# Background modulation steps of a hybrid encoder layer: from the gated recurrence's stage and the attention's projections to the first part of the output projection

## The chip, the core and the metric

The kernel runs on one core of a Trainium2 chip. A core has a matrix engine (TensorE, PE in the profile, with its weight loads listed apart as PEld), a vector engine (VectorE, DVE), an activation engine (ScalarE, ACT), a general engine (GpSimd, POOL) and a sync engine (SyncE, SP) that here only issues DMAs. The engines run side by side, each through its own instructions in order, and wait for each other by semaphores. The metric is the device time of one execution in microseconds; lower is better. A profile of one execution gives the start, length and waits of every instruction.

## The reference, cut to what matters

One encoder layer on 512 tokens of width 2048, in fp32. The input is modulated by a vector that is computed from a condition `c`, projected, mixed by four mixers of 512 channels each, projected back, and followed by a gated feed-forward network.

```
c_act = silu(c)
mod = c_act @ ada_w[l] + ada_b[l]                       # 2048 x 12288 weights, one row
shift1, scale1, gate1, shift2, scale2, gate2 = split(mod, 6)
h = x * (1 + scale1) + shift1
proj = h @ w_in[l]
o_a = _hgrn2(...)            # gated recurrence, 4 heads of 128
o_b = _s5(...)               # diagonal state space
o_c = _stick_breaking(...)   # attention, 4 heads of 128
o_d = _rwkv7(...)            # delta-rule recurrence, 8 heads of 64
mix = concatenate([o_a, o_b, o_c, o_d]) @ w_out[l]
x = layer_norm(ALPHA * x + gate1 * mix)
h = x * (1 + scale2) + shift2
ffn = (silu(h @ ffn_w1[l]) * (h @ ffn_w3[l])) @ ffn_w2[l]
x = layer_norm(ALPHA * x + gate2 * ffn)
```

The change concerns the part of `mod` that is needed late: `shift2` and `scale2`, which are used only when the feed-forward network begins.

## The kernel before, in words

**Matrix products.** Every fp32 product is done as three products of fp32r numbers: each operand is split into a high part (a cast on ACT, L102) and a low part (a subtraction on DVE, L105), and `mm3` (L592) adds high·high, low·high and high·low into one PSUM tile. A weight chunk is loaded by SP (`wr`), split into `wh` and `wl` by `wload` (L580), and used at once. A chunk of the projections is 128 rows by 512 columns; in the output projection it meets four token tiles, thus 12 matmuls of 128x512 for a chunk.

**Order.** The mixers' work and the projections are strung together by the string `ORDER` (L40). Each token names a piece of work. `K0` to `K3` are the attention's query and key projections of a head, `H0` to `H3` the heads of the gated recurrence, `L0` and `L1` the logarithms ahead of them, `VS` the attention's values, `A0` and `A1` its scores (tiles `sz`, `sl`, for two heads each), `TAIL` the end of the gated recurrence, `B0` and `B1` the attention's products with the values, `W1` and `W2` the first two parts of the output projection (`w_out`, L1420). A Tile scheduler places the instructions from this order, from priorities (`high_priority`, with 1500 ahead for the heads by `BEFORE`, L43, and 500 for the weight chunks, L582) and from its own estimate of when things are ready; so an instruction can stand well ahead of or behind its token.

**Background steps.** The product of `c_act` with three of the six parts of `ada_w` (in the order `gate1`, `scale2`, `shift2`, that is parts 2, 4, 3) is not a stage of its own. `ada_queue` (L1141) makes 12 items of it, a part's column block of 512 each. An item has 16 steps. A step loads a 128x512 tile `aw` of 256 KB (L1112, on SP's queue; the pool `ap` has three such tiles) and multiplies and adds it into `acc` on DVE (L123, or L118 for the first of an item). An item ends with `end` (L1123): it takes a PSUM tile `pd` from the four that the projections use too, does four matmuls of `acc` with a column of ones (128x1 each), and DVE writes the four columns into `mod`. This end is queued between later steps, at the tenth step of the item after the next, or behind ten empty entries for the last two. With them the queue has 224 entries.

**Rate.** The number behind the colon of a token is `E.rate`: so many entries of the queue are taken (`pump`, L1154) behind each weight chunk of that token (4 chunks for a feature tile, so 8 for `K0`; 16 for `VS`; 32 for `W1`, eight rows of `w_out` for each of four column blocks n). A load is issued up to three entries ahead. `PUMP` takes all that are left.

```
    while n and E.bg:
        for j in range(min(3, len(E.bg))):
            ld, do = E.bg[j]
            if ld:
                ld()
                E.bg[j] = (None, do)
        E.bg.pop(0)[1]()
        n -= 1
```

**The output projection.** `w_out` takes four PSUM tiles `pd` for a column block n, runs through the eight chunks, and then, for each token tile, DVE multiplies the PSUM tile by the gate (`go<-pd,g`) and adds it to the residual (`acc<-acc,go`). Since the pool has four `pd`, the next column block's matmuls wait for these `go`. Behind `W2` comes the last part, whose weights `wr` are loaded early, multiplied by the gate `g1` (L1468; `g1` lies in the pool `ap`, as `aw` does) and split (L1469).

Of the kernel before, what the change touches and what calls it, by code (L numbers as in the profile page):

```python
# [37 lines left out]
START = "M0 E0 G0 C0 g2 M1 S0 g6 F0 M2 S1 g1 E1"  # L38

ORDER = ("k3 xg:3 r1:1 v1 k2:1 v3 r3:3 v0:2 S5 r2 r0:1 KEYS SUB INV v2:3 V:1 R12:3 R4:3 CHAIN F2:1 F1:2 F3:1 "  # L40
         "R0:2 F0 K1:2 L0 H0 H1 K0:2 L1 H2 H3 VS:2 A0 K3:2 K2:2 PUMP TAIL B0 A1 W1:2 B1 W2")

BEFORE = {"S5": 600, "KEYS": 600, "SUB": 300, "INV": 1000, "CHAIN": 1500, "H": 1500}  # L43

# [1811 lines left out]
```

## Time and profile before

| | |
|---|---|
| three executions | 2540.97, 2546.42, 2553.87 us |
| median | 2546.42 us |
| the profiled execution, its own time | 2543.48 us |
| its span in the trace | 2541.5 us |
| granted TensorE clock, mean | 0.98 |
| instructions in the profile | 33306 |
| HBM read, written | 445.51 MB, 34.10 MB |

The profile's page gives busy time by engine, the span in 40 slices, and groups of instructions. Finer views of the same execution list single instructions in order of start (start and length in us, engine, line, operation, output<-inputs, and in square brackets the idle time just before and what ended it), or the busy time of each engine in chosen stretches. Matmuls are pipelined: a row of a matmul is listed with a length that overlaps the next one's start, so distances between starts tell its rate. The stretches that matter here are 712 to 834 us (the heads of the gated recurrence), 834 to 922 us (attention scores, the end of the recurrence, and the output projection's first column block) and 922 to 935 us (the step from its first to its second column block).

### The profile page before, as it was taken

The numbers are of one execution on the slowest core, as the hardware profiler recorded it, in microseconds if no ns is written. First come the engines' busy times: TensorE is split into PE (matmuls) and PEld (weight loads), VectorE is DVE, ScalarE is ACT, GpSimd is POOL, SyncE is SP. The second block draws the span as 40 slices with busy tenths as digits, with TensorE's granted clock in tenths as the row PEclk, the third lists the DMA queues.
The fourth block names the chain that finished last, engine by engine and source line by source line (L and its number), as shares of the span: only waits on it lengthen the run. The fifth ranks groups of instructions, "written<-read, shape, count | busy, mean of one in ns | idle before, by whom it ended". The sixth has DMA issues, their size and how long they took to land. (4 is left out here: it accounts for less than half of the span.)

```text
span 2541.5 us, 33306 instructions
## 1 busy us (share of the span) xinstructions
PE 2437.8 (96%) x11890; PEld 1897.7 (75%) x11890; DVE 1730.7 (68%) x2673; ACT 955.5 (38%) x1406; POOL 131.4 (5%) x293
## 2 busy tenths in 40 slices
PE   8999999999999999989999999999999999999996
PEld 3557767776788778867777877787778788788885
DVE  3755987357689975788787778777877744536227
ACT  2435242322454654164444444434443421121122
POOL 3300000010000000000000000000000000000000
PEclk9999999899999999999999999999999999999998
DMA  9876324334744554336666566655665788869632
GB/s 294 258 245 199 92 75 126 103 116 145 227 130 137 167 173 133 125 100 208 219 208 206 180 203 214 201 182 197 208 204 192 258 321 294 300 206 315 225 117 82
DMA packets 328877, 481.83 MB, mean 190 GB/s; under 512 B 44962, under 2 KB 151676, under 8 KB 328712
## 3 DMA queue, kind: packets, MB, share of 16 engines
q1 hardware_dynamic: 317976, 452.78, 55.3%
q0 software_dynamic: 8480, 26.27, 2.7%
q8 instruction: 93, 1.52, 0.3%
q10 hardware_dynamic: 2256, 0.67, 0.1%
q14 instruction: 72, 0.59, 0.1%
HBM read 445.51 MB, written 34.10 MB: 189 GB/s over the span
## 5 line engine op out<-in xcount | busy, mean ns | idle before, releaser
L102 ACT CAST wh<-wx 128x1024 fp32r<-128x1024 f32 (+1 forms) x416 | 401.2, 970 | 735.9 <-PE p L93 348.7
L105 DVE TENSOR_TENSOR wl<-wx,wh 128x1024 fp32r<-128x1024 f32 (+1 forms) x416 | 457.5, 1119 | 264.4 <-ACT wh L102 262.1
L102 ACT CAST wh<-wr 128x512 fp32r<-128x512 f32 x236 | 145.5, 618 | 329.2 <-PE pd L93 224.7
L123 DVE SCALAR_TENSOR_TENSOR acc<-aw,cact,acc 128x512 f32<-128x512 f32 x240 | 179.8, 749 | 123.6 <-DMA aw<-in_ada_w_dram 120.3
L93 PE MATMUL pt<-wl,gh 128*128 128x512 f32 x640 | 249.3, 390 | 2.1 <-DVE wl L105 1.8
L93 PE MATMUL pt<-wh,gh 128*128 128x512 f32 x640 | 249.1, 389 | 0.0
L93 PE MATMUL pt<-wh,gl 128*128 128x512 f32 x640 | 249.0, 389 | 0.0
L105 DVE TENSOR_TENSOR wx<-wx 128x512 f32<-128x512 f32 (+1 forms) x264 | 225.1, 866 | 28.6 <-DMA wx<-in_ffn_w_dram 26.9
L105 DVE TENSOR_TENSOR wl<-wr,wh 128x512 fp32r<-128x512 f32 x236 | 162.0, 689 | 113.3 <-ACT wh L102 96.2
L93 PE MATMUL pd<-hh,wl 128*128 128x512 f32 x512 | 205.6, 402 | 5.6 <-DVE wl L105 5.5
L93 PE MATMUL pd<-hh,wh 128*128 128x512 f32 x512 | 207.6, 407 | 2.4 <-ACT hh L102 2.4
L93 PE MATMUL pd<-hl,wh 128*128 128x512 f32 x512 | 204.0, 399 | 0.0
L93 PE MATMUL p<-wl,hdh 128*128 128x512 f32 x352 | 140.6, 404 | 20.0 <-DVE wl L105 20.0
L93 PE MATMUL p<-wh,hch 128*128 128x512 f32 x336 | 137.1, 408 | 16.4 <-DVE g L105 12.3
L93 PE MATMUL p<-wh,hdh 128*128 128x512 f32 x352 | 141.8, 403 | 1.1 <-ACT u L102 1.1
L93 PEld LDWEIGHTS pt<-wl,gh 128*128 128x128 f32 x640 | 120.1, 188 | 28.6 <-DVE wl L105 4.0
L93 PE MATMUL p<-wh,hdl 128*128 128x512 f32 x352 | 141.3, 402 | 0.0
L93 PEld LDWEIGHTS pt<-wh,gh 128*128 128x128 f32 x640 | 120.2, 188 | 25.6 <-ACT wh L102 0.8
L93 PEld LDWEIGHTS pt<-wh,gl 128*128 128x128 f32 x640 | 120.2, 188 | 25.1
L93 PE MATMUL p<-wl,hch 128*128 128x512 f32 x336 | 135.7, 404 | 0.3 <-DVE wl L105 0.3
L93 PE MATMUL p<-wh,hcl 128*128 128x512 f32 x336 | 135.0, 402 | 0.0
L93 PE MATMUL p<-wl,hbh 128*128 128x512 f32 x336 | 132.2, 393 | 0.8 <-DVE wl L105 0.8
(530 smaller groups left out, 4535.3 us busy)
## 6 DMA issues: line engine op xcount, KB each, us to landing
wx<-in_ffn_w_dram SPq DMA_DIRECT2D x592, 256.0 KB, 3.4
aw<-in_ada_w_dram SPq DMA_DIRECT2D x384, 256.0 KB, 4.6
wr<-in_w_in_dram SPq DMA_DIRECT2D x184, 256.0 KB, 3.3
wx<-in_ffn_w_dram SPq DMA_DIRECT2D x44, 1024.0 KB, 6.1
gh<-gd SPq DMA_DIRECT2D x88, 256.0 KB, 5.3
gl<-gd SPq DMA_DIRECT2D x88, 256.0 KB, 6.2
wr<-in_w_out_dram SPq DMA_DIRECT2D x64, 256.0 KB, 3.0
gd<-gh POOLq DMA_DIRECT2D x44, 256.0 KB, 4.1
```

What stands on the lines that cost most here:

```text
L93: return self.nc.tensor.matmul(out=out, lhsT=lhsT, rhs=rhs, start=start, stop=stop, **kw)
L102: self.nc.scalar.copy(out=out, in_=in_)
L105: self.nc.vector.tensor_tensor(out=out, in0=a, in1=b, op=op)
L123: self.nc.vector.scalar_tensor_tensor(out=out, in0=a, scalar=s, in1=b, op0=op0, op1=op1)
```

## The change

Only the string `ORDER` changes.

```diff
 ORDER = ("k3 xg:3 ... CHAIN F2:1 F1:2 F3:1 "
-         "R0:2 F0 K1:2 L0 H0 H1 K0:2 L1 H2 H3 VS:2 A0 K3:2 K2:2 PUMP TAIL B0 A1 W1:2 B1 W2")
+         "R0:2 F0 K1 L0 H0 H1 K0 L1 H2 H3 VS:1 A0 K3:1 K2:1 TAIL B0 A1 W1:4 PUMP B1 W2")
```

Up to `R0` both take 136 of the 224 entries. Before, `K1` and `K0` take 16 each, `VS` 32, `K3` 16, `K2` the last 8 (of 16 possible), so that `PUMP` and `W1` find the queue empty. After, `K1` and `K0` take none, `VS` 16, `K3` and `K2` 8 each, and the last 56 are taken by `W1`, four behind each of its first 14 chunks. These 56 are 32 steps with a load and a multiplication (the last two items, of `shift2`), the ends of four items, and 20 empty entries. `PUMP` finds nothing in either.

How the scheduler places it shows in the order of the instructions on each engine. The first place is DVE between the end of head 0 and the start of head 1 of the gated recurrence (`hS` and `ho` are head 0's last tiles, `hk`, `he`, `hlb` head 1's first, `acc<-aw` a background step, `wl` a weight chunk's low part). Before:

```order
L123 SCALAR_TENSOR_TENSOR acc_6611<-aw_6936,cact,acc_6611 128x512
L123 SCALAR_TENSOR_TENSOR hS_6753<-hS_6747,heb_6731,pm_6751 128x128
L123 SCALAR_TENSOR_TENSOR acc_6611<-aw_6939,cact,acc_6611 128x512
L123 SCALAR_TENSOR_TENSOR hS_6759<-hS_6753,heb_6731,pm_6757 128x128
L123 SCALAR_TENSOR_TENSOR acc_6611<-aw_6960,cact,acc_6611 128x512
L123 SCALAR_TENSOR_TENSOR ho_6763<-ho_6763,half_hg_norm_g,hgg_6402 128x512
L123 SCALAR_TENSOR_TENSOR acc_6611<-aw_6963,cact,acc_6611 128x512
L105 TENSOR_TENSOR wl_7045<-wr_7042,wh_7044 128x512
L123 SCALAR_TENSOR_TENSOR hk_6770<-hf_6016,he_6017 128x512
L123 SCALAR_TENSOR_TENSOR acc_6611<-aw_6984,cact,acc_6611 128x512
L123 SCALAR_TENSOR_TENSOR he_6017<-hf_6016,he_6017 128x512
L123 SCALAR_TENSOR_TENSOR acc_6611<-aw_6987,cact,acc_6611 128x512
```

The same place after:

```order
L105 TENSOR_TENSOR wl_6887<-wr_6884,wh_6886 128x512
L123 SCALAR_TENSOR_TENSOR hS_6701<-hS_6695,heb_6679,pm_6699 128x128
L123 SCALAR_TENSOR_TENSOR hS_6707<-hS_6701,heb_6679,pm_6705 128x128
L123 SCALAR_TENSOR_TENSOR ho_6711<-ho_6711,half_hg_norm_g,hgg_6402 128x512
L105 TENSOR_TENSOR wl_6905<-wr_6902,wh_6904 128x512
L123 SCALAR_TENSOR_TENSOR hk_6718<-hf_6016,he_6017 128x512
L123 SCALAR_TENSOR_TENSOR he_6017<-hf_6016,he_6017 128x512
L105 TENSOR_TENSOR hlb_6018<-hlb_6018,he_6017 128x512
L126 SCALAR_TENSOR_TENSOR hb_6724<-m_217,hlb_6018 128x512
```

The background steps between the head's instructions are gone, and the weight chunks' `wl` stand closer. Counted over the whole order on DVE, 28 background multiplications stand ahead of the first `hk` in the projections of `K1` and its neighbours before and 29 after, since the scheduler draws `VS`'s steps forward; about 32 stand among the four heads before and 3 after; about 17 stand from there to the second scores' `sz` before and 32 after; and from there none before and 16 after.

The second place is PE where `W1` goes from its first to its second column block (`pd` with `cath`, `catl` are the block's matmuls, each pair of `wh` and `wl` a weight chunk). Before:

```order
L93 MATMUL pd_8432<-wh_8561,cath_8411 128x512
L93 MATMUL pd_8432<-wh_8561,catl_8412 128x512
L93 MATMUL pd_8432<-wl_8562,cath_8411 128x512
L93 MATMUL pd_8603<-wh_8609,cath_8383 128x512
L93 MATMUL pd_8603<-wh_8609,catl_8384 128x512
L93 MATMUL pd_8603<-wl_8610,cath_8383 128x512
L93 MATMUL pd_8604<-wh_8609,cath_8383 128x512
```

And after, with the ends of two items and transposes of the scores (`pm<-ident,sz`) between:

```order
L93 MATMUL pd_8314<-wh_8535,cath_8293 128x512
L93 MATMUL pd_8314<-wh_8535,catl_8294 128x512
L93 MATMUL pd_8314<-wl_8536,cath_8293 128x512
L93 MATMUL pd_8400<-ones,acc_6395 128x1 x4
L96 MATMUL pm_9111<-ident,sz_8188 128x128 x4
L96 MATMUL pm_9118<-ident,sz_8189 128x128
L93 MATMUL pd_8527<-ones,acc_7657 128x1 x4
L93 MATMUL pd_8589<-wh_8595,cath_8265 128x512
L93 MATMUL pd_8589<-wh_8595,catl_8266 128x512
L93 MATMUL pd_8589<-wl_8596,cath_8265 128x512
L93 MATMUL pd_8589<-wh_8615,cath_8269 128x512
```

The two ends take the first two PSUM tiles that come free; the second block's first tile `pd_8589` now is the third to come free, where before its `pd_8603` was the first.

The third place is DVE at the same step, where the tiles come free. Before:

```order
L105 TENSOR_TENSOR go_8577<-pd_8429,g_1813_8427 128x512
L105 TENSOR_TENSOR go_8580<-pd_8430,g_1813_8427 128x512
L105 TENSOR_TENSOR acc_8415<-acc_8415,go_8577 128x512
L105 TENSOR_TENSOR wl_8646<-wr_8643,wh_8645 128x512
L105 TENSOR_TENSOR acc_8418<-acc_8418,go_8580 128x512
L105 TENSOR_TENSOR go_8583<-pd_8431,g_1813_8427 128x512
L105 TENSOR_TENSOR go_8586<-pd_8432,g_1813_8427 128x512
```

After, with the first two `go`, the end's `mod<-pd_8400` and a `wl` just ahead of these rows:

```order
L118 TENSOR_SCALAR acc_8462<-aw_8436,cact 128x512
L123 SCALAR_TENSOR_TENSOR mod<-pd_8527,c_148 128x4
L123 SCALAR_TENSOR_TENSOR acc_8462<-aw_8457,cact,acc_8462 128x512
L105 TENSOR_TENSOR acc_8297<-acc_8297,go_8563 128x512
L123 SCALAR_TENSOR_TENSOR acc_8462<-aw_8460,cact,acc_8462 128x512
L105 TENSOR_TENSOR acc_8300<-acc_8300,go_8566 128x512
L105 TENSOR_TENSOR go_8569<-pd_8313,g_1777_8309 128x512
L123 SCALAR_TENSOR_TENSOR acc_8462<-aw_8464,cact,acc_8462 128x512
L105 TENSOR_TENSOR acc_8303<-acc_8303,go_8569 128x512
L123 SCALAR_TENSOR_TENSOR acc_8462<-aw_8467,cact,acc_8462 128x512
L105 TENSOR_TENSOR go_8572<-pd_8314,g_1777_8309 128x512
```

The third and the fourth `go`, which free the second block's first two tiles, now stand behind two writes of `mod`, five background multiplications and three additions.

## The prediction

> **What bounds the kernel now.** I read the busy times of the engines first, then the busy time by stretch where the change works, then single instructions at the one place where PE stops.
>
> ```profile
> span 2541.5 us, 33306 instructions
> PE 2437.8 (96%) x11890; PEld 1897.7 (75%) x11890; DVE 1730.7 (68%) x2673; ACT 955.5 (38%) x1406; POOL 131.4 (5%) x293
> ```
>
> PE is busy for 96% of the span; a microsecond can be won only where PE idles or runs slowly, and is lost where the change makes PE wait. The sum is made against this execution's own time, 2543.48 us, of which 2541.5 are the span; the median of the three is 2.9 higher. The stretches (for each engine busy us and instructions, then granted clock, DMA share, GB/s):
>
> ```profile
> core 0: us, PE busy (x) PEld busy (x) DVE busy (x) ACT busy (x) POOL busy (x), PEclk, DMA share, GB/s
> 656.00:672.00 16.00, 13.52 (x57) 10.47 (x58) 10.70 (x18) 7.30 (x11) 0.00 (x0) 1.00 0.78 233
> 712.00:834.00 122.00, 119.94 (x697) 101.47 (x696) 109.02 (x214) 55.73 (x122) 1.58 (x3) 1.00 0.42 122
> 834.00:900.00 66.00, 63.69 (x309) 49.40 (x308) 58.91 (x107) 43.90 (x77) 0.00 (x0) 1.00 0.60 184
> 900.00:922.00 22.00, 21.90 (x97) 17.64 (x96) 19.95 (x37) 17.76 (x29) 0.00 (x0) 1.00 0.65 213
> 922.00:935.00 13.00, 7.86 (x25) 6.02 (x24) 10.18 (x20) 4.97 (x9) 0.00 (x0) 0.74 0.43 142
> 935.00:1040.00 105.00, 105.00 (x492) 86.96 (x491) 61.28 (x97) 39.64 (x68) 0.00 (x0) 1.00 0.38 123
> ```
>
> While the heads run (712 to 834), DVE is busy for 109 of 122 us, yet PE idles only 2.06. From 834 to 900 PE idles 2.31. From 935 on it does not idle at all. The loss is in 922 to 935, between `W1`'s first and second column block; PE there:
>
> ```profile
> 921.98 0.39 PE L93 MATMUL pd<-wl,cath 128*128 128x512 f32 x1
> 927.51 0.76 PE L93 MATMUL pd<-wh,cath 128*128 128x512 f32 x1 [5.14 <-ACT sz L99]
> 928.08 0.63 PE L93 MATMUL pd<-wh,catl 128*128 128x512 f32 x1
> ...
> 931.92 0.50 PE L93 MATMUL pd<-wh,catl 128*128 128x512 f32 x1
> 932.26 0.39 PE L93 MATMUL pd<-wl,cath 128*128 128x512 f32 x1
> 932.48 0.39 PE L93 MATMUL pd<-wh,cath 128*128 128x512 f32 x1
> ```
>
> PE waits 5.14 us and then runs at half rate: eleven starts, 927.51 to 932.26, take 4.75 us where at 0.227 each (932.26 to 932.48, like the rows before the pause) they would take 2.50, so 2.25 more are lost. The releaser is given as ACT's `sz`, but the rows of DVE show what came last:
>
> ```profile
> 920.15 2.36 DVE L126 TENSOR_TENSOR_SCAN sl<-ones,sl 128x512 f32<-128x512 f32 x3
> 922.47 0.69 DVE L105 TENSOR_TENSOR sz<-sz,sl 128x512 f32<-128x512 f32 x1
> 923.07 0.69 DVE L105 TENSOR_TENSOR wl<-wr,wh 128x512 fp32r<-128x512 f32 x1
> 923.67 2.50 DVE L105 TENSOR_TENSOR sz<-sz,sl 128x512 f32<-128x512 f32 x4
> 926.08 0.69 DVE L105 TENSOR_TENSOR wl<-wr,wh 128x512 fp32r<-128x512 f32 x1
> 926.68 1.29 DVE L105 TENSOR_TENSOR go<-pd,g 128x512 f32<-128x512 f32 x2
> ```
>
> The `go` that frees the first PSUM tile stands behind the scores' `sl` and `sz`, and 0.83 us after its start (926.68 to 927.51) the second block starts. DVE operations of 0.69 start 0.60 apart (922.47, 923.07, 923.67).
>
> **The change part by part.** No multiplication, load or end is removed; 192 stay 192 over the kernel. So only places count.
>
> *1. The serial chain between the column blocks.* After, the second block's first two tiles are the third and fourth to come free, because two ends take the first two. The prices:
>
> ```profile
> 708.79 0.95 PE L93 MATMUL pd<-ones,acc 128*128 128x1 f32 x8
> L96 PE MATMUL pm<-ident,sz 128*128 128x128 f32 x20 | 2.5, 272 | 0.0
> L123 DVE SCALAR_TENSOR_TENSOR mod<-pd,c 128x4 f32<-128x4 f32 x8 | 1.3, 158 | 2.2 <-PE pd L93 2.2
> L123 DVE SCALAR_TENSOR_TENSOR acc<-aw,cact,acc 128x512 f32<-128x512 f32 x28 | 20.9, 747 | 0.0
> L118 DVE TENSOR_SCALAR acc<-aw,cact 128x512 f32<-128x512 f32 x2 | 1.0, 482 | 0.0
> ```
>
> An end is 0.95 on PE (its four matmuls leave eight records) and 0.16 on DVE; five transposes are 2.5/20 x 5 = 0.6; a multiplication is 0.75, started 0.66 apart by the overlap above. A hand-over between the engines is 0.83 - 0.69 = 0.14. Counted from the start of the first `go`: the first end runs on PE 0.83 to 1.78; its `mod` on DVE 1.92 to 2.08; `wl` to 2.68; the first multiplication to 3.16. On PE the transposes run to 2.38, the second end to 3.33, so its `mod` to 3.63. Then two multiplications (1.32), two `acc` (1.20), the third `go` (0.69) and the hand-over (0.14): the second block starts at 7.0 instead of 0.83, 6.2 later. The two ends and the transposes (2.5) are work that PE had to do elsewhere before, where it is saturated, so **+3.7** net. Its second tile needs the fourth `go`, which ends two multiplications, one `acc` and itself behind the third: 1.32 + 0.60 + 0.60 = 2.5 later, while PE has five matmuls for the first tile (1.1): **+1.4**. The multiplications wait for loads as well, in order on DVE:
>
> ```profile
> DMA to landing us min/median/max: 2.6/3.5/4.6
> 668.40 0.75 DVE L123 SCALAR_TENSOR_TENSOR acc<-aw,cact,acc 128x512 f32<-128x512 f32 x1 [2.06 <-DMA aw<-in_ada_w_dram]
> ```
>
> With three tiles in the pool, the tile of the fourth multiplication is loaded once the first is done (3.16) and read at 7.0 - 0.14 = 6.9, 3.7 later: a load of 2.6 or 3.5 is in time, one of 4.6 adds 0.9. I leave it at 0, bounds 0 and +1.
>
> *2. The clock behind this pause.* Half rate behind the pause cost 2.25. A longer pause may cost the same again (0), or the ends and transposes are also at half rate and the ten matmuls behind the second wait too (2.5 + 2.25 = 4.7). What shows that a short pause does not count:
>
> ```profile
> 714.14 1.10 PE L93 MATMUL pm<-hx 128*128 128x64 f32 x8 [1.98 <-DVE hx L105]
> ```
>
> This pause of 1.98 lies in a stretch with a granted clock of 1.00. The second wait is 1.4, so it should be free by itself; I take **+1.5**, nearer to nothing, bounds 0 and +4.7. The Trainium skill, page "TensorE: Matmul & The Clock Gate", section "Part 1: The HAM clock gate (the "warmup" mystery)", has an activity window of about 3.4 us that runs free, at whose end an idle array falls to half rate and a busy one returns to full; the rows agree (5.14 us slowed it, 1.98 did not, and it came back after 4.75). By that rule the sum would lie between nothing and one further window.
>
> *3. The step from the second to the third block.* There the last two ends take the first two tiles. By the same prices: first `mod` to 2.08, `acc` to 2.68, second end on PE to 2.73, its `mod` to 3.03, `acc` to 3.63, third `go` to 4.32, hand-over 4.46, against 0.83; less 1.9 of ends: **+1.7**, bounds 0 (PE finds other matmuls) and +1.7. In the trace of before PE does not idle here (the row from 935).
>
> *4. The scores' stage, 834 to 922.* Some 32 multiplications instead of 17 stand there.
>
> ```profile
> L123 DVE SCALAR_TENSOR_TENSOR acc<-aw,cact,acc 128x512 f32<-128x512 f32 x17 | 12.7, 749 | 2.2 <-DMA aw<-in_ada_w_dram 2.2
> L123 DVE SCALAR_TENSOR_TENSOR acc<-aw,cact,acc 128x512 f32<-128x512 f32 x11 | 8.2, 750 | 5.3 <-DMA aw<-in_ada_w_dram 5.0
> L105 DVE TENSOR_TENSOR wr<-wr,g 128x512 f32<-128x512 f32 x9 | 6.1, 689 | 1.9 <-DMA wr<-in_w_out_dram 1.9
> ```
>
> These rows are the multiplications of 834 to 900, those of 656 to 672, and the gated weights of the last part in 900 to 922. Where 17 multiplications waited 2.2 us for loads, PE idled 2.31, or 0.136 each; where 11 waited 5.0, it idled 2.48, or 0.225 each. Behind a waiting multiplication stand the `wl` that PE needs. Fifteen more cost 15 x 0.136 = **+2.0**, bounds 0 and 15 x 0.225 = +3.4. In return the nine gated-weight operations (6.1 us of DVE) leave the stretch ahead of the pause, since `g1` shares the pool `ap` and comes only after the last background tile. That lets the first `go` start sooner, by 4.45 at most (5.14 less the `go` itself); but the chain `sl`, `sz` sets the pause, and more multiplications compete, so **-1**, bounds -4.5 and 0. The gated weights land in the third block, where DVE has 61 of 105 us filled: no cost.
>
> *5. The heads.* Some 29 multiplications (29 x 0.66 = 19 us) leave DVE there. PE idled 2.06 there, so that is the most to be won. Against it: without fillers each head's levels come in pairs as only head 1's did before, and
>
> ```profile
> 746.00:764.00 18.00, 17.92 (x114) 15.64 (x114) 16.09 (x36) 7.81 (x20) 0.53 (x1) 1.00 0.18 52
> ```
>
> head 1 had 17.92 of 18.00 on PE, so that pattern feeds PE as well. Should it fail, a pause like that at 714.14 in each of the three other heads is 3 x 1.98 = +5.9. I take **-0.5**, bounds -2.1 and +5.9. `K1` is not relieved, since 29 multiplications stand there instead of 28.
>
> *Sum:* 3.7 + 1.4 + 1.5 + 1.7 + 2.0 - 1.0 - 0.5 = +8.8, so 2543.48 + 8.8 = **2552** (2555 from the median). All terms at their low ends, with 5.1 for the chain, give 5.1 - 4.5 - 2.1 = -1.5; all at their high ends 6.1 + 4.7 + 1.7 + 3.4 + 5.9 = +21.8.
>
> **The rivals.** *The relieved DVE arrives in time:* the scores' chain runs early, the first `go` comes as the first block ends, and 5.14 + 2.25 + 2.06 are won while the new chain stays (5.1 + 1.7): -2.7, 2541. If PE also fills that chain with other matmuls, it is -9.5, 2534. For it speaks 109 busy us of 122 on DVE; against it, that PE idles only 2.06 in that stretch, and that the multiplications reappear in the scores' stage just ahead of the pause. Chance 0.15, a third of it for the second form.
>
> *The loads set the pace (the slower side):* with three tiles `aw`, a step cannot be shorter than a load and its multiplication by three: (3.5 + 0.75)/3 = 1.42. `W1` takes more than one step in a chunk of 12 x 0.227 = 2.72; from two a chunk (2.84) DVE, in order, falls behind, and the `wl` behind it stop PE. At the 0.225 per multiplication of 656 to 672 the 48 moved into the scores' stage and `W1` cost 48 x 0.225 = 10.8 instead of 2.0: 2561. For it, the waits in these rows; against it, 17 multiplications with 0.136 each. Chance 0.2.
>
> *The change does nothing:* the scheduler spreads steps to where DVE has room, as 29 for 28 ahead of head 0 shows, and what PE loses at the blocks it wins at the heads: 2543.5. Chance 0.15.
>
> *The clock stays low for a second window:* only five matmuls (1.1 us) lie between the two pauses of step 1, and PE keeps half rate over another 4.75 us and once more behind the third block's step: 2.25 + 2.25 instead of 1.5, 2555. The Trainium skill's free-running window (same page and section) would allow it. Chance 0.1.
>
> **How the numbers follow.** The forecast has 0.4. The range takes in the first rival at 2541 and, nearly, the sum at its high ends (2565): 2540 to 2566; 0.05 lie below and about 0.1 above. A measurement of this kernel can tell 0.5%, 12.7 us, from no change: faster means under 2531, slower over 2556. Faster: a part of the second form of the first rival, 0.04. Slower: most of the loads' rival (0.17) and the upper tails of the forecast and the clock (0.08), 0.25. The same: 0.71.
>
> **What would show it.** Between `W1`'s first and second block, the ends `pd<-ones,acc` and two gaps on PE, some 7 us from the first `go` to the next block, and a granted clock under 0.74 in 13 us around it; two ends and a gap of about 1.7 a block later; no gap beyond 2 us among the heads, at about the same length from the first `hk` on; 0.136 lost per multiplication in the scores' stage, with waits for `aw`. Wrong would be: the first `go` no longer behind `sz`; gaps of `wl` behind `aw` all through `W1`; or the heads' stage shorter by more than 2 us.

## The result and the profile after

| | before | after | ratio, 95% interval |
|---|---|---|---|
| first comparison, median | 2546.17 us (6 runs) | 2567.35 us (6 runs, 2558.24 to 2572.92) | 1.0076, 1.0057 to 1.0096 |
| second comparison, median | 2548.97 us (17 runs) | 2567.92 us (5 runs) | 1.0071, 1.0059 to 1.0084 |
| profiled execution, its own time | 2543.48 us | 2570.09 us | |

The changed kernel is slower by 0.7 to 0.8%, 19 to 21 us. The head of its page:

```profile
span 2568.2 us, 33298 instructions
PE 2456.6 (96%) x11890; PEld 1913.6 (75%) x11890; DVE 1733.0 (67%) x2673; ACT 954.7 (37%) x1406; POOL 131.3 (5%) x293
```

DVE has the same 2673 instructions and as much busy time; PE has the same number and is listed as busy for 18.8 us more. To say where the time came from I cut the trace at the starts of named instructions on PE (the first and last `hx` product, the first matmul of each column block of `W1`). Stretches hold different work, since the scheduler moves projections between them. So the table also has **PE's loss**: a stretch's length less the sum, over its matmuls, of the median distance from a start to the next start for that shape (0.227 us for 128x512), taken from the kernel before. Each kernel was traced twice; the second trace stands behind the comma.

| stretch | length before | after | matmuls before, after | loss before | loss after |
|---|---|---|---|---|---|
| heads (first to last `hx`) | 111.5 | 94.2 | 635, 538 | 3.6, 5.2 | 7.5, 8.8 |
| scores' stage (to `W1`) | 65.3 | 89.5 | 311, 385 | 1.9, 1.5 | 7.5, 6.8 |
| block 1 (to the second block) | 36.6 | 39.6 | 152, 173 | 7.0, 6.3 | 7.6, 7.2 |
| block 2 | 24.0 | 33.8 | 96, 123 | 2.2, 1.4 | 9.0, 10.3 |
| block 3 | 21.9 | 23.5 | 96, 96 | 0.1, 0.1 | 1.7, 1.8 |
| block 4 | 23.6 | 21.9 | 112, 96 | 0.1, 0.0 | 0.1, 0.1 |
| sum | 282.9 | 302.6 | | 14.9, 14.5 | 33.4, 35.0 |

The loss grows by 18 to 20 us in these six stretches, which is nearly the whole difference of the medians. About half of it is idle time of PE as listed (9.6 and 8.5 us in the two traces before, 19.9 and 20.7 after); the rest is work at half rate (4.6 and 6.2 us of work before, 23.2 and 25.1 after). What the profiled executions differ by beyond it (26.6 us) lies ahead of the heads and in the feed-forward network, where the two traces of one kernel differ as much: from the network's first to its second part 937.0 and 942.4 us in two traces of the kernel before, 943.1 and 939.9 after. Single traces of a stretch agree within about 2 us.

The same view by stretch as in the prediction, after (for each engine busy us and instructions, then granted clock, DMA share, GB/s):

```profile
core 0: us, PE busy (x) PEld busy (x) DVE busy (x) ACT busy (x) POOL busy (x), PEclk, DMA share, GB/s
717.00:812.00 95.00, 92.82 (x540) 77.76 (x541) 79.36 (x161) 46.18 (x104) 1.58 (x3) 0.98 0.16 48
812.00:901.00 89.00, 83.23 (x384) 66.42 (x383) 67.44 (x119) 45.10 (x78) 0.00 (x0) 0.97 0.55 164
933.00:945.00 12.00, 8.22 (x33) 7.36 (x34) 9.50 (x19) 3.86 (x7) 0.00 (x0) 0.72 0.39 123
945.00:965.00 20.00, 20.00 (x93) 16.52 (x92) 13.71 (x21) 5.62 (x10) 0.00 (x0) 1.00 0.76 249
965.00:980.00 15.00, 9.48 (x38) 8.09 (x36) 7.62 (x14) 1.69 (x4) 0.00 (x0) 0.66 0.67 201
```

DVE is relieved among the heads (79 of 95 us, where it had 109 of 122), and yet the clock is 0.98 there. The second trace of the kernel before has 0.98 in this stretch as well (714.5 to 827.6), so this figure does not come from the change alone (see the last section). The two steps between blocks have 0.72 and 0.66, where only one stretch with 0.74 was before. PE at the first step:

```profile
932.52 0.39 PE L93 MATMUL pd<-wl,cath 128*128 128x512 f32 x1
936.78 1.51 PE L93 MATMUL pd<-ones,acc 128*128 128x1 f32 x8 [3.88 <-DVE go L105]
938.15 1.31 PE L96 MATMUL pm<-ident,sz 128*128 128x128 f32 x5
939.25 1.71 PE L93 MATMUL pd<-ones,acc 128*128 128x1 f32 x8
940.82 0.77 PE L93 MATMUL pd<-wh,cath 128*128 128x512 f32 x1
```

And DVE there:

```profile
936.05 1.28 DVE L105 TENSOR_TENSOR go<-pd,g 128x512 f32<-128x512 f32 x2
938.33 0.16 DVE L123 SCALAR_TENSOR_TENSOR mod<-pd,c 128x4 f32<-128x4 f32 x1 [1.00 <-PE pd L93]
940.99 0.16 DVE L123 SCALAR_TENSOR_TENSOR mod<-pd,c 128x4 f32<-128x4 f32 x1 [1.50 <-PE pd L93]
943.60 0.68 DVE L105 TENSOR_TENSOR go<-pd,g 128x512 f32<-128x512 f32 x1
```

The second block starts at 940.82, 4.77 us after the first `go` (0.83 before): it follows the second end at once and does not wait for the third `go` of 943.60. At the second step:

```profile
965.08 0.60 PE L96 MATMUL pm<-ident,sz 128*128 128x128 f32 x4
971.20 3.57 PE L93 MATMUL pd<-ones,acc 128*128 128x1 f32 x16 [5.52 <-DVE go L105]
974.63 0.77 PE L93 MATMUL pd<-wh,cath 128*128 128x512 f32 x1
```

```profile
964.11 0.75 DVE L123 SCALAR_TENSOR_TENSOR acc<-aw,cact,acc 128x512 f32<-128x512 f32 x1 [0.86 <-DMA aw<-in_ada_w_dram]
966.79 0.75 DVE L123 SCALAR_TENSOR_TENSOR acc<-aw,cact,acc 128x512 f32<-128x512 f32 x1 [1.33 <-DMA aw<-in_ada_w_dram]
970.45 1.29 DVE L105 TENSOR_TENSOR go<-pd,g 128x512 f32<-128x512 f32 x2 [2.31 <-DMA g<-gate]
973.10 0.16 DVE L123 SCALAR_TENSOR_TENSOR mod<-pd,c 128x4 f32<-128x4 f32 x1 [1.36 <-PE pd L93]
```

and SP's own queue, whose issues go out in order:

```profile
962.27 0.43 SPq L1112 DMA_DIRECT2D aw<-in_ada_w_dram  x1
962.75 0.43 SPq L1426 DMA_DIRECT2D acc<-in_x_dram  x1
965.49 0.33 SPq L584 DMA_DIRECT2D wr<-in_w_out_dram  x1
965.86 0.43 SPq L1168 DMA_DIRECT2D g<-gate  x1
```

This is one chain through three queues. DVE waits for `aw`, in order, so `wl` behind it is late; SP's next weight load `wr` waits for the buffer that this `wl` frees; the gate's broadcast `g` stands behind that `wr` on SP and goes out at 965.86; the `go` waits for it until 970.45, the ends for the `go`, the next block for the ends. Before, the same `g` went out at 936.08 for a `go` at 950.07.

In the scores' stage PE's transposes wait for `ho`:

```profile
897.06 4.53 PE L96 MATMUL pm<-ident,sz 128*128 128x128 f32 x20 [4.57 <-DVE ho L105]
```

```profile
892.00 0.74 DVE L123 SCALAR_TENSOR_TENSOR acc<-aw,cact,acc 128x512 f32<-128x512 f32 x1
892.66 0.68 DVE L105 TENSOR_TENSOR catl<-oT,cath 128x512 fp32r<-128x512 f32 x1
893.26 0.68 DVE L105 TENSOR_TENSOR wl<-wr,wh 128x512 fp32r<-128x512 f32 x1
893.86 0.68 DVE L105 TENSOR_TENSOR catl<-oT,cath 128x512 fp32r<-128x512 f32 x1
894.47 0.74 DVE L123 SCALAR_TENSOR_TENSOR acc<-aw,cact,acc 128x512 f32<-128x512 f32 x1
```

and the `ho` comes at 896.33. Between 880 and 896 about every third operation of DVE is a background multiplication, among them steps of items that the queue hands out only in `W1`: the scheduler drew them up here. The first of the two last items starts with this row:

```profile
879.40 0.48 DVE L118 TENSOR_SCALAR acc<-aw,cact 128x512 f32<-128x512 f32 x1
```

So of this stage's 29 multiplications 16 belong to the item ahead of the last two, and 13 to the late entries. Before, the same transposes waited 1.32 and 0.73.

### The profile page after: what moved, and what is told of

It reads as the page before. It is cut to its first block, busy times and chain, and to the rows that moved or that the text cites. A ratio compares the mean times of both kernels' runs of the same rounds, so it can differ in the third digit from the quotient of the medians.

```text
span 2568.2 us, 33298 instructions
## 1 busy us (share of the span) xinstructions
PE 2456.6 (96%) x11890; PEld 1913.6 (75%) x11890; DVE 1733.0 (67%) x2673; ACT 954.7 (37%) x1406; POOL 131.3 (5%) x293
## 5 line engine op out<-in xcount | busy, mean ns | idle before, releaser
L93 PEld LDWEIGHTS pt<-wh,gh 128*128 128x128 f32 x640 | 120.1, 188 | 25.7 <-ACT wh L102 0.8
```

The source lines that it names most:

```text
L93: return self.nc.tensor.matmul(out=out, lhsT=lhsT, rhs=rhs, start=start, stop=stop, **kw)
```

## The experiments

All kernels below are compared with the kernel before, run beside them. Loss is given as heads, scores' stage, blocks 1 to 4, and sum; before has 3.6, 1.9, 7.0, 2.2, 0.1, 0.1, sum 14.9. Letters of theories are those of the expectations.

| kernel | median us (before beside it) | ratio, 95% interval | heads | scores | 1 | 2 | 3 | 4 | sum |
|---|---|---|---|---|---|---|---|---|---|
| after again | 2567.92 (2548.97) | 1.0071, 1.0059 to 1.0084 | 8.8 | 6.8 | 7.2 | 10.3 | 1.8 | 0.1 | 35.0 |
| gate early | 2567.68 (2544.99) | 1.0092, 1.0071 to 1.0113 | 8.8 | 6.7 | 7.2 | 5.1 | 2.7 | 0.1 | 30.6 |
| ends on `pm` | 2559.72 (2544.99) | 1.0060, 1.0038 to 1.0082 | 7.4 | 7.3 | 5.3 | 3.6 | 0.8 | 0.5 | 24.9 |
| no late entries | 2539.53 (2544.99) | 0.9979, 0.9961 to 0.9997 | 6.5 | 1.0 | 5.3 | 1.7 | 0.1 | 0.1 | 14.7 |
| late entries only | 2557.34 (2544.99) | 1.0041, 1.0021 to 1.0060 | 5.3 | 1.7 | 7.2 | 10.9 | 1.7 | 0.1 | 26.9 |
| `TAIL` first | 2566.59 (2548.97) | 1.0071, 1.0058 to 1.0085 | 10.5 | 4.5 | 7.6 | 10.8 | 2.0 | 0.1 | 35.5 |
| late from block 2 | 2553.26 (2548.97) | 1.0021, 1.0008 to 1.0033 | 5.7 | 1.7 | 5.3 | 5.3 | 3.4 | -0.1 | 21.3 |
| three edits | 2564.67 (2548.97) | 1.0061, 1.0048 to 1.0074 | 7.4 | 9.5 | 5.4 | 4.0 | 0.6 | 0.7 | 27.6 |
| all late | 2569.91 (2547.55) | 1.0084, 1.0065 to 1.0104 | 9.0 | 0.8 | 5.3 | 3.1 | 4.5 | 17.2 | 39.9 |
| front | 2571.16 (2547.55) | 1.0095, 1.0074 to 1.0116 | 5.2 | 25.7 | 5.3 | 1.7 | 0.1 | 0.0 | 38.0 |
| four tiles | 2555.84 (2547.55) | 1.0025, 1.0011 to 1.0039 | 5.2 | 4.2 | 7.6 | 4.9 | 1.7 | 0.1 | 23.7 |

The kernel before and the changed one were each traced a second time, for the scatter:

> The kernel before, unchanged, for a second trace. All theories: PE's loss by stage as in the first (a stretch's length less the sum of its matmuls' median distances from start to start): 3.6 us from first to last hx, 1.9 from there to the first matmul of W1, 7.0 to the second block, 2.2 to the third, 0.1 to the fourth, each within 2.

> The changed kernel unchanged, for a second trace of it and beside the others of this call. All theories: 18 to 24 us over before. By stage, if the first trace is typical: first hx to first matmul of W1 183 to 185 us (before 176.8), from there to the second block 39 to 40 (36.6), to the third 33 to 35 (24.0), to the fourth 23 to 24 (21.9).

Both came as expected (losses in the table of the result); the one time of the kernel before was 2547.99.

**The gate's broadcast early.**

```diff
-            g1 = bcast(E, E.gate[2][0:1, T * n : T * n + T], "g1")
+            with tc.high_priority(offset=500):
+                g1 = bcast(E, E.gate[2][0:1, T * n : T * n + T], "g1", "w1")
```

> The changed kernel, but the gate's broadcast g of a column block gets a buffer of its own and is queued ahead on SP. In the changed kernel's trace the second block's g is issued at 965.86, behind the background loads and the fifth weight chunk of the block after, and the go waits for it until 970.45, 5.4 us after the block's last matmul. Theory A (g queued late on SP costs what it shows): the wait of 5.4 us between the second and third block goes, with it up to 2 us of half rate; 5 to 7 us under the changed kernel, 2560 to 2562. Theory B (the background loads set the pace in W1, and g is only what was named last): another wait takes its place, under 2 us gained, 2565 to 2568.

Block 2 loses 5.1 instead of 9.0 and 10.3, block 3 one more. The median does not show it; 3 to 4 us are within what the two comparisons leave open. DVE at the second step of this kernel shows what took part of the place:

```profile
965.89 0.68 DVE L105 TENSOR_TENSOR go<-pd,g 128x512 f32<-128x512 f32 x1
967.83 0.75 DVE L123 SCALAR_TENSOR_TENSOR acc<-aw,cact,acc 128x512 f32<-128x512 f32 x1 [1.26 <-DMA aw<-in_ada_w_dram]
968.50 0.68 DVE L105 TENSOR_TENSOR wl<-wr,wh 128x512 fp32r<-128x512 f32 x1
```

The first `go` is in time now, and the end behind it waits, in order on DVE, for a multiplication whose tile has not landed. By the time, B holds. Of A, the wait for `g` went as expected, but another one took most of its place.

**The ends on other PSUM tiles.**

```diff
-        ps = E.psd()
+        ps = E.psm() if (part, b) in ((4, 3), (3, 0), (3, 1), (3, 2), (3, 3)) else E.psd()
```

> The changed kernel, but the ends of the last five items take a PSUM tile pm instead of one of the four pd that the output projection uses. Theory A (the ends stand in the serial chain between the column blocks): the first go to the next block's first matmul takes 0.8 to 2 us instead of 4.8, and the step from the second to the third block is shorter by 2 to 3.4 although it still waits for g; 5 to 8 us gained, 2559 to 2562. Theory B (the multiplications and their loads ahead of the go set it, not the PSUM tiles): the first go comes later by what is won, under 2 us gained, 2565 to 2568.

8.5 to 10 us of loss go, and about 8 us of the median. The first step of this kernel, on DVE and PE:

```profile
932.38 1.28 DVE L105 TENSOR_TENSOR go<-pd,g 128x512 f32<-128x512 f32 x2
```

```profile
933.20 0.77 PE L93 MATMUL pd<-wh,cath 128*128 128x512 f32 x1 [4.01 <-DVE go L105]
```

The `go` to the block is 0.82 again, as before the change. Theory A holds for the ends: they cost as long as they share the four tiles of the output projection. The edit did a little more than that: 8 and 12 multiplications stand in blocks 1 and 2 instead of 4 and 15, and at the second step the first `go` (958.21) comes ahead of the block's last matmul (959.24), so the wait for `g`, which theory A expected to stay, is gone too.

**Without the late entries, and with them alone.** The first leaves out the last two items and the last four ends, so that `shift2` is zero; the second leaves the heads as before and nothing for the scores' tokens.

```diff
+    del E.bg[168:]
+    E.nc.vector.memset(E.mod[:, 48:64], 0.0)
```

> The changed kernel without the queue's last 56 entries, those that W1 takes: the last two items (32 loads and multiplications) and four ends are left out, and shift2 is set to zero. So W1 is as before the change, and what is left is the move among the heads and the scores. Theory A (about 7 us of the loss lie there: from the first hx to the first matmul of W1 176.8 us before and 183.8 after): 5 to 8 us over before, 2551 to 2554. Theory C (the loss is all in W1; the 7 us are the scatter of one execution, or multiplications of the last 56 that float up into the scores' stage): within 2 us of before or below it, 2543 to 2548.

```diff
-         "R0:2 F0 K1 L0 H0 H1 K0 L1 H2 H3 VS:1 A0 K3:1 K2:1 TAIL B0 A1 W1:4 PUMP B1 W2")
+         "R0:2 F0 K1:2 L0 H0 H1 K0:2 L1 H2 H3 VS A0 K3 K2 TAIL B0 A1 W1:4 PUMP B1 W2")
```

> The rates K1:2 and K0:2 as before, none for VS, K3 and K2, and W1:4: the heads keep their background steps, and the same 56 entries as in the changed kernel are left for W1. Theory A (13 us in W1, 7 among the heads and the scores): W1's loss stays and the other is gone, 11 to 15 us over before, 2557 to 2561. Theory C (all in W1): 18 to 22 us over before, 2564 to 2568.

Without the late entries nothing is lost against before (14.7 to 14.9), though the rates of the other tokens are the changed ones; 32 loads and multiplications are missing, so this is not the same work. Theory C was right here, and the time even lies below its range. Alone, the late entries cost 12 us, 8.7 of them in block 2; only 7 multiplications stand in the scores' stage, and it loses 1.7. There A's range held, and C's did not.

Whether the late entries also make the loss of the scores' stage is not shown. Without them the stage has no multiplication at all and loses 1.0. But the 16 of the item ahead of them have left it as well: they stand at the beginning of the heads and among them (14, where the changed kernel has none). What the changed kernel's trace shows is that the longest wait, that for `ho`, stands right behind nine multiplications of the late entries.

**`TAIL` ahead of the multiplications.**

```diff
-        hg_tail(E, O, GG, RS)
+        with tc.high_priority(offset=300):
+            hg_tail(E, O, GG, RS)
```

> The changed kernel, but the instructions of TAIL have a priority of 300, so that its ho stand ahead of the background multiplications on DVE and not behind them. Theory D (the loss ahead of W1 is the wait of 4.6 us of PE's transposes for ho, and the half rate behind it, both from multiplications ahead of ho): first hx to first matmul of W1 177 to 179 us instead of 183.8, the pause between ho and the transposes at most 2 us; in total 4 to 7 us gained, 2560 to 2563. Theory E (the multiplications cost by their number and by waits for their loads wherever they stand in the scores' stage): that stretch stays above 181 us, or what is won is lost before the second block; under 2 us gained.

The scores' stage loses 4.5 instead of 7.5 and 6.8, but nothing is left of it at the end (heads 10.5, in the same order as in the changed kernel; 5.1 of it is half rate). By the time, E's range held. The wait for `ho` is gone; a new one stands earlier, since the priority also moved `TAIL`'s matmuls forward on PE:

```profile
869.15 1.14 PE L93 MATMUL pm<-rs,selC 32*128 32x512 f32 x8 [2.74 <-DVE rs L105]
```

So the edit changed two engines, and D is neither shown nor excluded by it; that a reorder of DVE alone would win the 3 to 5 us was not tried.

**All three edits together.**

> The changed kernel with its own rates and all three edits: gate's broadcast early in a buffer of its own, ends on pm, TAIL with a priority of 300. Theory A with D (these three make up the loss): 14 to 19 us gained over the changed kernel, 2548 to 2553, so 2 to 7 us over before. Theory B with E (the in-order multiplications and their loads find another wait): less than 10 us gained.

Theory A with D missed; 3 us gained lie within B with E. Blocks 1 and 2 behave as with the ends on `pm`, but `TAIL`'s matmuls, now ahead on PE, wait 6 us for `ho`:

```profile
873.83 2.07 PE L93 MATMUL pm<-rs,selC 32*128 32x512 f32 x2 [6.24 <-DVE ho L105]
```

and the scores' stage loses 9.5. The edits do not add up; with the ends alone the kernel is faster.

**Late entries from the second block on**, with the ends on `pm`, the rates of the late-entries-alone kernel, and this:

```diff
-                pump(E, E.rate)
+                pump(E, E.rate if n else 0)
```

> The same 56 late entries in W1 at four a chunk, but only from its second column block on, the ends on pm tiles, the heads with their steps as before the change (K1:2, K0:2), and none for VS, K3 and K2. So no multiplication stands in the scores' stage or around the first step between blocks; they stand where DVE had 11.8 of 24 and 11 of 22 us filled. Theory A with D (place decides, not number): first hx to W1 174 to 176 us, second block at 35 to 37 from there, third 24 to 26, fourth 22 to 24; in total 4 to 0 us below before, 2541 to 2546. Theory B with E (multiplications in W1 cost by their waits for loads): 4 to 10 us over before.

4 to 5 us over before instead of at or below it: A with D missed, B with E came. The heads lose 5.7 (1.7 of it half rate; 3.6 and 5.2 before), the scores' stage and block 1 no more than before, but blocks 2 and 3, with 11 and 5 multiplications, lose 8.7 instead of 2.3. DVE had room there, but it waits 4.5 us for `aw`, the `go` behind one such wait comes late, and PE pauses 2.08 us ahead of block 3. The rest of what is lost there is half rate: two spells of 6.83 us, where the kernel before has one.

**All 88 entries late**, from the second block on, ends on `pm`, no rate for `K1`, `K0`, `VS`, `K3`, `K2`:

> No background step for K1, K0, VS, K3 and K2: all 88 entries are left for W1, four a chunk from its second block on, the ends on pm tiles. So neither the heads nor the scores' stage have multiplications, and W1's second to fourth block have 11, 14 and 23. Theory F (heads without fillers lose by themselves): PE's loss from first to last hx is 7 to 9 us as in the changed kernel (7.5 and 8.8), against 3.6 to 5.7 in kernels whose heads keep their steps. Theory G (it is the scatter of single executions): 3.5 to 5.7. For the scores' stage all theories: 1 to 2. For the blocks: if each multiplication there costs the 0.3 to 0.4 us that e9's two blocks show, 14 to 19 us; if those were ends and half rate, 6 to 9. Total 5 to 20 us over before.

The total is 22 us over before, above what was expected, since blocks 2 to 4 lose 24.8. The heads lose 9.0 with nothing added near them, as theory F had it; 3.4 of it is half rate, to which the last section comes back. In block 4 PE stands at the last end:

```profile
1019.11 1.84 PE L93 MATMUL pm<-ones,acc 128*128 128x1 f32 x8 [10.69 <-DVE acc L123]
```

```profile
1010.85 1.54 DVE L123 SCALAR_TENSOR_TENSOR acc<-aw,cact,acc 128x512 f32<-128x512 f32 x2 [1.87 <-DMA aw<-in_ada_w_dram]
1014.73 0.75 DVE L123 SCALAR_TENSOR_TENSOR acc<-aw,cact,acc 128x512 f32<-128x512 f32 x1 [1.08 <-DMA aw<-in_ada_w_dram]
1017.42 1.54 DVE L123 SCALAR_TENSOR_TENSOR acc<-aw,cact,acc 128x512 f32<-128x512 f32 x2 [1.94 <-DMA aw<-in_ada_w_dram]
```

The end stands on PE where the scheduler thought that its item would be done; the multiplications come at the pace of the loads and are not.

**More of it ahead**, from the kernel before:

```diff
-         "R0:2 F0 K1:2 L0 H0 H1 K0:2 L1 H2 H3 VS:2 A0 K3:2 K2:2 PUMP TAIL B0 A1 W1:2 B1 W2")
+         "R0:2 F0 K1:3 L0 H0 H1 K0:3 L1 H2 H3 VS:3 A0 K3 K2 PUMP TAIL B0 A1 W1 B1 W2")
```

> The kernel before with the rates K1:3, K0:3 and VS:3, nothing for K3 and K2: 33 multiplications among the heads instead of 29, 16 instead of 20 in the scores' stage, none in W1. Theory A with D (place decides, and before W1 only a crowd ahead of ho costs): within 2 us of before, 2543 to 2549. Theory H (DVE is full among the heads, so that four more are paid in full): 2 to 5 us over before.

Far off: 24 us over before, and neither theory's mechanism. PE stands at an end as in the last kernel, now in the scores' stage:

```profile
865.10 1.87 PE L93 MATMUL pd<-ones,acc 128*128 128x1 f32 x8 [13.65 <-DVE acc L123]
```

The end again stands on PE well ahead of its item's last multiplication. Here the loads are only a small part of the reason: from 838 to 866 DVE waits 1.5 us for `aw`. The multiplications stand, in order, between the operations of the scores, and most start 1.1 to 1.6 us apart.

**Four tiles `aw`** in the changed kernel, with loads issued four entries ahead:

```diff
-        st[k] = E.ap.tile([128, T], F32, name=E.nm("aw"), tag="aw")
+        E.turn = getattr(E, "turn", 0) + 1
+        p, tag = (E.w1, "t") if E.turn % 4 == 0 else (E.ap, "aw")
+        st[k] = p.tile([128, T], F32, name=E.nm("aw"), tag=tag)
```

> The changed kernel with four tiles aw instead of three and loads issued four entries ahead, the order on PE and DVE kept. Theory B (the loads of the three tiles set the pace, so that multiplications in order on DVE hold up wl, ho and go): waits of DVE for aw from the heads' end to the third block fall to less than half, 4 to 8 us gained on the changed kernel, 2559 to 2563. Theory A (the gate's late broadcast, the ends and the order on DVE): under 2 us gained, 2565 to 2568.

Theory B: 12 us less in the median than the changed kernel, and a loss of 23.7 instead of 33.4 and 35.0, more than expected. DVE's idle time ahead of the multiplications (us, times), from 640 us to the end of the late entries, in the kernel before, the changed one and the one with four tiles:

```profile
  DMA aw<-in_ada_w_dram: 18.1, 19
```

```profile
  DMA aw<-in_ada_w_dram: 26.5, 34
```

```profile
  DMA aw<-in_ada_w_dram: 12.6, 17
```

Scores' stage 4.2 instead of 7.5, block 2 4.9 instead of 9.0 with a pause of 1.70 in place of 5.52. The heads lose 5.2 instead of 7.5 and 8.8; that this trace has no half rate there, where the two of the changed kernel have 1.7 and 3.1 us of loss by it, is the larger part of this and is not the loads' doing as far as is shown. Block 1, where the ends are the chain, is not changed (7.6).

No version that does all the work beat the kernel before. The kernel before with four tiles, which these numbers suggest (it waits 18.1 us for `aw` itself), was not run.

## Why the prediction was right or wrong

The direction was right, the size was not: +8.8 us forecast, 19 to 21 measured; 2567.35 lies just over the range's upper end (2566), and slower by more than 0.5%, which came, had a chance of 0.25. Step by step, in PE's loss:

1. *The serial chain, forecast +3.7 and +1.4, with +1.5 for the clock and -1 for an earlier `go`: 5.6 together; measured +0.6 and +0.9 in two traces.* The step that failed is "the second block's first two tiles are the third and fourth to come free": an end hands its tile on when its `mod` is read out, so the block started 4.77 and not 7.0 after the first `go`, without a second wait. The first tile that came free again was the first end's, not the third `go`'s. The rest held: the first `go` came 3.5 after the block's last matmul instead of 4.7, and half rate lasted as long as before or longer (6.83 us before and after in the first traces, 3.41 and 10.24 in the second). Part of it falls into block 2: with that part (2.2 and 1.4 us before, 1.6 and 2.3 after) the step costs 0 to 1.8 us more than before.
2. *The second step, forecast +1.7; measured +6.8 to +8.9.* Less the half rate of the first step that runs on into this block, it is +7.4 to +8.0. This is the term that was sized most wrongly. The prediction priced the ends only. It took `go` as ready and did not look at what `g` stands behind on SP; 5.4 us lie between PE's last work of the block (965.08) and the `go` (970.45). The edit of `g` alone took about 4 to 5 off this block's loss, the ends alone 5 to 7, four tiles 4 to 5. These are links of one chain, and their shares overlap.
3. *Block 3, "no cost"; measured +1.6.* Its first matmuls run at half rate behind that pause.
4. *The scores' stage, forecast +2.0; measured +5.3 to +5.6.* The price of 0.136 for a multiplication came from a stretch where they were spread; here they stood in a crowd ahead of `ho`, with waits for their loads (no run removed the crowd and left the rest as it is). A price for each instruction was the wrong form: by the trace, the stage loses 1.7 with 7 multiplications (late entries only), 1.9 with 22 (before) and 7 with 29 (after).
5. *The heads, forecast -0.5; measured +3.6 to +3.9.* The sign failed. Relieving DVE won nothing: PE's one long wait there, for the first `hx` from DVE, grew from 1.98 and 1.42 us to 3.06 and 3.07, and its idle time in the stretch from 2.1 and 1.5 to 4.7 and 4.8. So the order without fillers lost by a pause, as the high end (+5.9) had it, though by one at the first `hx` and not by 1.98 in each head. The rest is half rate, 1.7 and 3.1 us of loss against 0 and 1.7 before. In the seven traces with three tiles and no multiplication among the heads the first `hx` waits 3.06 to 3.23 and PE idles 4.7 to 4.9; with four tiles it waits 2.60, PE idles 3.7, the clock stays at 1.00, and the heads lose 5.2. Why the wait is longer there stays open; no run changed it alone.

The prediction also named a heads' stage shorter by more than 2 us as a sign of being wrong. It is shorter by 17 us, but because 97 matmuls of the projections moved out of it; the loss in it grew.

Of the rivals, the one of the loads (0.2, 2561) is what the runs bear out best: four tiles took back more than half. It is not the whole, since the ends on `pm`, which leave the tiles `aw` as they are, took back 8 us, and the two gains were not tried together. The relieved DVE did not arrive in time (the first `go` still stands behind `sz`), and the change did not do nothing. The clock's rival is true as a part: half rate now stands at four places (first `hx`, the transposes behind `ho`, both steps between blocks).

## What to carry to other kernels

Before a load with its step is moved, compare its pace (buffers, time to land) with the pace at which the new place takes it, and look at every instruction that stands behind it on all three queues: DVE's `wl`, SP's next loads, PE's end of the item. An engine's idle share in the new place says nothing of that. A step's closing work that takes a buffer of the main loop is priced by when that buffer is handed on, which is best read from who reads it last.

## What the runs showed of the hardware that was not expected

The length of a pause alone does not decide whether PE comes back at half rate. That 1.98 us did not slow the clock, as the prediction read it, is true of that trace and not in general. The wait before the first `hx` with four tiles, in the changed kernel and with the late entries only:

```profile
711.62 1.10 PE L93 MATMUL pm<-hx 128*128 128x64 f32 x8 [2.60 <-DVE hx L105]
```

```profile
717.49 1.10 PE L93 MATMUL pm<-hx 128*128 128x64 f32 x8 [3.06 <-DVE hx L105]
```

```profile
712.32 1.62 PE L93 MATMUL pm<-hx 128*128 128x64 f32 x8 [1.79 <-DVE hx L105]
714.27 0.63 PE L93 MATMUL pd<-hl,wh 128*128 128x512 f32 x1
```

After 2.60 (and 1.98, and 2.06 in the kernel with more of it ahead) the granted clock of the heads is 1.00. After 3.06, but also after 1.79, and after 1.42 in the second trace of the kernel before, matmuls of 128x512 are listed with 0.63 instead of 0.39, and the heads' clock is 0.98. What the traces show instead is a grid. In each of the 14 traces every change of the granted clock lies a whole number of cells of 3.413 us from every other (to within 5 ns), so half rate lasts 3.41, 6.83 or 10.24 us and so on. Two cells of this grid around the pause, with the late entries only and with four tiles (columns as in the tables by stretch):

```profile
709.31:712.73 3.42, 1.63 (x10) 1.06 (x8) 3.42 (x7) 0.72 (x2) 0.00 (x0) 1.00 0.54 159
712.73:716.14 3.41, 3.41 (x13) 2.93 (x12) 2.63 (x7) 1.71 (x5) 0.00 (x0) 0.50 0.55 152
```

```profile
707.54:710.96 3.42, 1.48 (x7) 0.90 (x5) 2.93 (x5) 2.52 (x7) 0.00 (x0) 1.00 0.30 93
710.96:714.37 3.41, 2.75 (x19) 2.48 (x20) 3.08 (x9) 1.95 (x6) 0.00 (x0) 1.00 0.25 75
```

Over all 14 traces, a cell at full clock in which PE is listed as busy for less than 40% was followed by half rate each time (197 of 197); with 40 to 60%, 38 of 92 were; above that, 16 of 9577. So a pause that fills one cell costs, and the same pause split between two may not. What decides in the middle is not shown. The Trainium skill, page "TensorE: Matmul & The Clock Gate", section "Part 1: The HAM clock gate (the "warmup" mystery)", has a free-running window of about 3.4 us and a fall to half rate after an idle one. The grid agrees with it; here the clock also fell after a cell with PE busy for 1.63 of 3.42 us. Short pauses with thin work between them did it too: with the gate early, pauses of 1.35 and 0.34 around the ends, whose matmuls are 128x1, were followed by twelve matmuls 0.43 apart:

```profile
969.31 1.40 PE L93 MATMUL pd<-ones,acc 128*128 128x1 f32 x8 [1.35 <-DVE mod L123]
971.06 0.76 PE L93 MATMUL pd<-wh,cath 128*128 128x512 f32 x1 [0.34 <-DVE mod L123]
```

So in single traces some microseconds of half rate come and go with where the grid lies; they are part of the scatter of about 2 us in a stretch.
